# First-norm columns of a decoder layer built by VectorE and through DRAM instead of by TensorE

## The chip, the cores and the metric

One core of one Trainium2 chip runs the whole kernel. The metric is the device time of one execution in microseconds. TensorE (PE) multiplies matrices, VectorE (DVE) and ScalarE (ACT) do the elementwise work, GpSimd (POOL) does a little, and SyncE's queue (SP) issues most transfers. Each engine takes its instructions in the order in which they were written for it, and a waiting instruction holds up all behind it. PE's weight loads are shown as PEld.

## What is computed

One decoder layer over 1024 tokens of 1024 channels, in float32:

```python
z = x @ w_in                                   # pool group | q | k | v
mix = concat(pool_mixer(z), attention(z)) @ w_out
h = layer_norm(ALPHA * x + mix, ln1_g, ln1_b)  # the first norm
ff = square(relu(h @ w_ff1)) @ w_ff2           # hidden width 4096
h = layer_norm(ALPHA * h + ff, ln2_g, ln2_b)
out = h + sigmoid(h @ w_ple_gate + b) * (p @ w_ple)
```

The result of the first norm is used twice: as the residual, with tokens in rows, and as input of `w_ff1`, where the contraction runs over channels. The product wants it in columns: channels on the 128 partitions, tokens along the free axis.

## The kernel before

Each float32 product is made of three matmuls of the reduced type fp32r (lines 113 to 115): an operand is split into a high part (ScalarE, `high`, line 98) and the rest (VectorE, `low`, line 103).

The tokens stand in eight tiles of 128 rows, `hn[0]` to `hn[7]`. For each tile the residual and the products with `w_out` come first (`out_left`, `out_right`, `residual`, line 440), then `norm1(n)`. This normalizes the tile in place (`layer_norm`, lines 402 to 419: its last two steps are L418 and L118 on 128x1024), turns it into columns with eight TensorE transposes of 128x128 into two PSUM banks (`transposed`, line 427; tiles `pt` and `av`), stores ALPHA times the rows to DRAM for later (lines 532 and 533, `hd`), and builds the operands of the feed-forward products from the columns.

The product with `w_ff1` is done by a scheme of seven block products in place of eight (Strassen's, in Winograd's form). Its right operands, over all 1024 tokens, are seven tiles of columns: "11" and "21" are the columns of tiles 0 to 3 (channels 0 to 511 and 512 to 1023); "22", "T1", "T2", "T3" are made from the columns of tiles 4 to 7 and of those; "T4" comes last (`last_sum`). The profile calls "11", "21", "T1", "T2", "T3", "T4" all `c` and "22" `x`; with numbers they are c_335, c_336, c_374, c_375, c_376, c_377 and x7_373. Each is 512 tokens wide, so a matmul on one needs the columns of all four token tiles.

The order around the change: TensorE does `out_left(1)`, the four `out_right` of tiles 4 to 7 (24 matmuls each), then sixteen products of twelve matmuls on "11" and "21" (`early(0)` to `early(7)`: one on "11" and, later, one on "21" for each), and then the main loop, whose first matmuls are on "T2" (PSUM tiles `f`). `norm1(4)` to `norm1(7)` are written between the `early` calls. Within dependences and a bounded set of buffers a scheduler sets each engine's order when the kernel is built. The buffers that matter: `ws` (six of 4 KB per partition: raw weights and their split parts), `w` (two: raw weights), `n` (eight of 4 KB: `hn` and others).

Each of the weight blocks for these products comes by a transfer on SP's queue (line 583 for `early`, 639 for the main loop), is split by ScalarE and VectorE into `ws`, and then loaded as the stationary operand.

Of the kernel before, what the change touches and what calls it, by code (L numbers as in the profile page):

```python
# [67 lines left out]
def layer(ctx, tc, xT, x, pT, w_in, w_pool, pscale, sinks, w_out, ln1, w1, w2, ln2, w_ple, w_gate, bgate, bias, rcount, out):  # L68
    nc = tc.nc
# [6 lines left out]
    def nm(s):  # L76
        uid[0] += 1
        return f"{s}_{uid[0]}"
# [7 lines left out]
    def nat(shape, dt=F32):  # L86
        return sb.tile(shape, dt, tag="n", bufs=8, name=nm("n"))
# [8 lines left out]
    def high(dst, src, scale=None):  # L96
        if scale is None:
            nc.scalar.copy(out=dst, in_=src)  # L98
        else:
            nc.scalar.mul(out=dst, in_=src, mul=scale)  # L100

    def low(eng, dst, src, hi):
        return eng.tensor_tensor(out=dst, in0=src, in1=hi.bitcast(F32), op=ALU.subtract)  # L103
# [13 lines left out]
    def add(o, a, b, op=ALU.add):  # L117
        nc.vector.tensor_tensor(out=o, in0=a, in1=b, op=op)  # L118
# [13 lines left out]


    h_dram = [tc.dram_tile([P, D], F32, name=f"hd{n}") for n in range(NT)]
    f_dram = [tc.dram_tile([P, 2, 2, 2, HALF], F32, name=f"fd{q}") for q in range(NQUAD - NKEEP)]


# [3 lines left out]
    ps = ps_ctx.enter_context(tc.tile_pool(name="ps", bufs=1, space=PSUM))  # L141
# [26 lines left out]
    def tr_ps():  # L168
        return ps.tile([P, 4, P], F32, tag="pt", bufs=2, name=nm("pt"))
# [227 lines left out]
    hn = [None] * NT  # L397

    def layer_norm(y, gb, root=False):
        st = small([P, 2, 6])  # L400
        for i in range(2):
            nc.vector.bn_stats(out=st[:, i, :], in_=y[:, i * HALF : (i + 1) * HALF])
        mv = small([P, 8])
        nc.vector.bn_aggr(out=mv[:, 0:2], in_=st.rearrange("p a b -> p (a b)"))
        v, r0, e, r, m = (mv[:, i : i + 1] for i in range(2, 7))
        nc.vector.tensor_scalar(out=v, in0=mv[:, 1:2], scalar1=LN_EPS, scalar2=None, op0=ALU.add)
        if root:
            nc.vector.reciprocal(out=r0, in_=v)
            nc.scalar.activation(out=r0, in_=r0, func=AF.Sqrt)
        else:  # L410
            nc.gpsimd.tensor_tensor(out=r0, in0=v, in1=mhalf, op=ALU.pow)

        nc.vector.scalar_tensor_tensor(out=e, in0=r0, scalar=v, in1=r0, op0=ALU.mult, op1=ALU.mult)
        nc.vector.tensor_scalar(out=e, in0=e, scalar1=-0.5, scalar2=1.5, op0=ALU.mult, op1=ALU.add)
        nc.vector.tensor_tensor(out=r, in0=r0, in1=e, op=ALU.mult)
        nc.vector.tensor_scalar(out=m, in0=mv[:, 0:1], scalar1=-1.0, scalar2=None, op0=ALU.mult)
        nc.scalar.activation(out=y, in_=y, func=AF.Identity, bias=m, scale=1.0)
        nc.vector.scalar_tensor_tensor(out=y, in0=y, scalar=r, in1=gb[0], op0=ALU.mult, op1=ALU.mult)  # L418
        add(y, y, gb[1])

    def tr_av():
        return ps.tile([P, 4, P], F32, tag="av", bufs=1, name=nm("av"))

    def transposed(y, j, pt):
        for k in range(4):
            kt = 4 * j + k
            nc.tensor.transpose(pt[:, k, :], y[:, kt * P : (kt + 1) * P], ident)  # L427
        return pt
# [77 lines left out]
    def temp(shape=(P, HALF)):  # L506
        return p1.tile(list(shape), F32, tag="t", bufs=6, name=nm("t"))

    def part(shape=(P, 2, 4, P), dt=F32R):
        return p1.tile(list(shape), dt, tag="ws", bufs=6, name=nm("ws"))  # L510

    def wide(tag, shape, dt):
        return p1.tile(shape, dt, tag=tag, bufs=1, name=nm(tag))


    X = {}

    def block(name, i, c):
        return X[name][:, i, :, c * P : (c + 1) * P].bitcast(F32)

    def split_to(name, c, src, eng):
        cs = slice(c * P, (c + 1) * P)
        dh = X[name][:, 0, :, cs]
        high(dh, src)
        return low(eng, X[name][:, 1, :, cs], src, dh)

    def norm1(n):
        t, c = n // 4, n % 4
        layer_norm(hn[n], gb1)
        a = transposed(hn[n], 0, tr_ps())  # L530
        b = transposed(hn[n], 1, tr_av())
        nc.scalar.mul(out=hn[n], in_=hn[n], mul=ALPHA)
        nc.scalar.dma_start(out=h_dram[n], in_=hn[n])
        if t == 0:
            if c < 3:
                nc.scalar.copy(out=pre[:, 4 + c].rearrange("p (k t) -> p k t", k=4), in_=a)
            split_to("11", c, a, nc.vector)
            split_to("21", c, b, nc.vector)
        else:
            r12, t1, t2 = temp((P, 4, P)), temp((P, 4, P)), nat([P, 4, P])  # L540
            nc.scalar.copy(out=r12, in_=a)
            if c < 3:
                add(t1, a, pre[:, 4 + c].rearrange("p (k t) -> p k t", k=4), ALU.subtract)
# [191 lines left out]
    for i in range(len(order) + AHEAD):  # L735
# [9 lines left out]
        p, name = order[i - AHEAD]  # L745
# [91 lines left out]
    for u, (i, q) in enumerate(units):  # L837
        k = QORDER.index(q)
# [133 lines left out]
```

## Time and profile before

| what | value |
| --- | --- |
| median of three timed runs | 994.76 us (994.67 to 995.08) |
| the profiled execution: span from first to last instruction | 993.0 us |
| lies around the span, against the median | 1.8 us |
| PE, DVE, ACT, POOL busy | 985.4, 711.0, 457.9, 105.6 us |
| granted TensorE clock | 1.000 |
| DMA moved | 148.01 MB |

The profiled execution has no time of its own beside its span; the three timed runs agree within 0.04%, so its time is taken as the median, 1.8 us above the span. Busy time is an engine's time in instructions, and idle time of an engine that nothing waits for costs nothing. A row of the timeline gives start, duration, engine, line, operation, tiles and shapes; neighbouring starts on PE are closer than the durations since matmuls overlap in the pipeline.

### The profile page before, as it was taken

What the parts mean: (1) busy time and instruction counts of PE and PEld (TensorE: products, weight loads), DVE (VectorE), ACT (ScalarE), POOL (GpSimd) and SP (SyncE); (2) the same over time, 40 slices, a digit from 0 to 9 for tenths busy, and PEclk for the clock granted to TensorE, in tenths of its full rate; (3) what the DMA queues carried; (4) which work ended last, traced back from release to release, by engine and by line L of the source; (5) the groups of instructions that cost most, each with busy time, mean ns of one, the idle gap of its engine ahead of it and who ended that gap; (6) DMA issues with size and microseconds to landing.
All of it is one profiled execution on the core that took longest, in us unless ns stands there. A gap on an engine that the chain in (4) does not pass through costs nothing.

```text
span 993.0 us, 12231 instructions
## 1 busy us (share of the span) xinstructions
PE 985.4 (99%) x4562; PEld 820.8 (83%) x4562; DVE 711.0 (72%) x1137; ACT 457.9 (46%) x737; POOL 105.6 (11%) x142
## 2 busy tenths in 40 slices
PE   9999999999999999999999999999999999999998
PEld 7888887888888888888888888888888888888887
DVE  5898888895869777564446756887647799896333
ACT  5676766543576443434444434433343454651111
POOL 0013562020000000100000000100111010000000
PEclk9999999999999999999999999999999999999999
DMA  6512142722161543742372993675798863721011
GB/s 218 181 64 85 45 147 85 233 82 89 66 238 57 191 149 149 198 163 106 118 274 96 343 330 101 181 227 201 207 212 186 217 157 118 215 73 43 35 40 43
DMA packets 39004, 148.01 MB, mean 149 GB/s; under 512 B 4768, under 2 KB 5920, under 8 KB 36128
## 3 DMA queue, kind: packets, MB, share of 16 engines
q1 hardware_dynamic: 29520, 115.90, 34.2%
q0 software_dynamic: 7840, 26.74, 11.4%
q10 hardware_dynamic: 1584, 4.59, 1.1%
q8 instruction: 36, 0.59, 0.2%
q14 instruction: 24, 0.20, 0.1%
HBM read 124.66 MB, written 22.54 MB: 148 GB/s over the span
## 4 chain that ended last, share of the span: by engine, by line
PE 98%; DVE 1%; POOL 1%; DMA 0%; issue 0%; ACT 0%; DVEq 0%
PE f L114 23%; PE f L115 23%; PE f L113 23%; PE mm L113 8%; PE mm L115 8%; PE mm L114 8%; PE pt L316 1%; PE s L293 1%; PE s L292 1%; PE f L427 1%; PE av L321 1%; PE av L322 1%; POOL h L360 0%; PE s L113 0%; PE s L114 0%; DMA n<-in_xT 0%
## 5 line engine op out<-in xcount | busy, mean ns | idle before, releaser
L113 PE MATMUL f<-c,ws 128*128 128x512 f32 (+1 forms) x456 | 175.8, 385 | 0.0
L114 PE MATMUL f<-c,ws 128*128 128x512 f32 (+1 forms) x456 | 175.7, 385 | 0.0
L115 PE MATMUL f<-c,ws 128*128 128x512 f32 (+1 forms) x456 | 175.2, 385 | 0.0
L115 PE MATMUL f<-x,w 128*128 128x512 f32 x448 | 174.3, 389 | 0.0
L114 PE MATMUL f<-x,w 128*128 128x512 f32 x448 | 174.3, 389 | 0.0
L113 PE MATMUL f<-x,w 128*128 128x512 f32 x448 | 147.1, 389 | 0.0
L98 ACT CAST w<-st 128x1024 fp32r<-128x1024 f32 (+2 forms) x66 | 65.7, 998 | 109.0 <-issue 69.9
L103 DVE TENSOR_TENSOR w<-st,w 128x1024 fp32r<-128x1024 f32 (+2 forms) x66 | 77.5, 1177 | 48.9 <-ACT w L98 48.8
L113 PEld LDWEIGHTS f<-c,ws 128*128 128x128 f32 x456 | 85.7, 188 | 17.2
L114 PEld LDWEIGHTS f<-c,ws 128*128 128x128 f32 x456 | 85.7, 188 | 17.1
L115 PEld LDWEIGHTS f<-c,ws 128*128 128x128 f32 x456 | 85.7, 188 | 17.1
L115 PEld LDWEIGHTS f<-x,w 128*128 128x128 f32 x448 | 84.1, 188 | 17.5
L114 PEld LDWEIGHTS f<-x,w 128*128 128x128 f32 x448 | 84.1, 188 | 17.5
L113 PEld LDWEIGHTS f<-x,w 128*128 128x128 f32 x448 | 84.0, 188 | 17.4
L98 ACT CAST ws<-w 128x512 fp32r<-128x512 f32 x60 | 37.1, 622 | 57.5 <-PE f L115 42.4
L103 DVE TENSOR_TENSOR x<-ws,x 128x1024 fp32r<-128x1024 f32 x52 | 63.4, 1218 | 0.0
L118 DVE TENSOR_TENSOR n<-t,f 128x512 f32<-128x512 f32 x48 | 31.9, 685 | 39.3 <-PE f L115 39.2
L103 DVE TENSOR_TENSOR ws<-w,ws 128x512 fp32r<-128x512 f32 x60 | 41.1, 689 | 25.1 <-ACT ws L98 24.7
L98 ACT CAST ws<-st 128x512 fp32r<-128x512 f32 x48 | 29.8, 621 | 60.1 <-PE f L115 35.2
L113 PE MATMUL mm<-c,w 128*128 128x512 f32 x144 | 56.4, 396 | 0.3 <-ACT w L98 0.3
L115 PE MATMUL mm<-c,w 128*128 128x512 f32 x144 | 56.5, 394 | 0.0
L114 PE MATMUL mm<-c,w 128*128 128x512 f32 x144 | 56.4, 393 | 0.0
(212 smaller groups left out, 1819.5 us busy)
## 6 DMA issues: line engine op xcount, KB each, us to landing
ws<-in_w SPq DMA_DIRECT2D x70, 512.0 KB, 3.9
w<-in_w SPq DMA_DIRECT2D x16, 1024.0 KB, 5.3
c<-fd SPq DMA_DIRECT2D x6, 2048.0 KB, 8.4
fd<-n POOLq DMA_DIRECT2D x20, 512.0 KB, 3.5
ws<-in_w POOLq DMA_DIRECT2D x20, 512.0 KB, 7.8
st<-in_w_in SPq DMA_DIRECT2D x17, 512.0 KB, 3.3
w<-in_w SPq DMA_DIRECT2D x10, 512.0 KB, 4.1
n<-in_x SPq DMA_DIRECT2D x8, 512.0 KB, 6.0
```

The source lines that it names most:

```text
L98: nc.scalar.copy(out=dst, in_=src)
L103: return eng.tensor_tensor(out=dst, in0=src, in1=hi.bitcast(F32), op=ALU.subtract)
L113: nc.tensor.matmul(o, ah, bh, start=first, stop=False, skip_group_check=more)
L114: nc.tensor.matmul(o, ah, bl, start=False, stop=False, skip_group_check=more)
L115: nc.tensor.matmul(o, al, bh, start=False, stop=last, skip_group_check=more)
L118: nc.vector.tensor_tensor(out=o, in0=a, in1=b, op=op)
L292: nc.tensor.matmul(s[:, i, dst], ql, kt[:, 0, g, kk : kk + kn], start=True, stop=False)
L293: nc.tensor.matmul(s[:, i, dst], ql, kt[:, 1, g, kk : kk + kn], start=False, stop=True)
L316: nc.tensor.transpose(pt[:, i, :], e[:, i, kb * P : (kb + 1) * P], ident)
L321: nc.tensor.matmul(av, VV[0][:, blk, g], pp[:, 0], start=(kb == lo), stop=False)
L322: nc.tensor.matmul(av, VV[0][:, blk, g], pp[:, 1], start=False, stop=(kb == 1))
L427: nc.tensor.transpose(pt[:, k, :], y[:, kt * P : (kt + 1) * P], ident)
```

## The change

`norm1` no longer calls `transposed`. In its place stands `flip`: VectorE transposes the tile in 32x32 pieces in one instruction (128x1024, into a `ws` buffer), SP's queue stores the result to a DRAM scratch (`td0` to `td7`, 512 KB each, 4 KB per partition), and four transfers on the same queue, one for each group of 32 partitions (128 KB each, in runs of 1 KB), read it back in the order that makes columns. The four reads wait for the store. They land in another `ws` buffer for tiles 0 to 3 and in an `n` buffer for tiles 4 to 7. All that read the columns in PSUM now read them there, in views of four by 32 tokens (4x4x32). The second norm (`gate_in`) keeps its TensorE transposes.

```diff
+    t_dram = [tc.dram_tile([P, 4, 2 * P], F32, name=f"td{n}") for n in range(2 * NT)]
...
-    def tr_av():
-        return ps.tile([P, 4, P], F32, tag="av", bufs=1, name=nm("av"))
+    def flip(y, b, t, d):
+        b4 = b.rearrange("p (q k c) -> p q k c", q=4, k=NK)
+        nc.vector.transpose(out=b4, in_=y.rearrange("p (k q r) -> p q k r", k=NK, q=4))
+        nc.sync.dma_start(out=d, in_=b.rearrange("p (q e) -> p q e", q=4))
+        for q in range(4):
+            nc.sync.dma_start(
+                out=t[32 * q : 32 * q + 32].rearrange("r (R e) -> r R e", R=4),
+                in_=d[:, q].rearrange("(R r) e -> r R e", R=4),
+            )
+        return t.rearrange("p (R k c) -> p R k c", R=4, k=NK)
...
+    def columns(name, i, c):
+        return X[name][:, i, :, c * P : (c + 1) * P].rearrange("p k (R c) -> p R k c", R=4)
...
     def norm1(n):
         t, c = n // 4, n % 4
         layer_norm(hn[n], gb1)
-        a = transposed(hn[n], 0, tr_ps())
-        b = transposed(hn[n], 1, tr_av())
+        ft = flip(hn[n], part((P, D), F32), nat([P, D]) if t else part((P, D), F32), t_dram[n])
+        a, b = ft[:, :, 0:4], ft[:, :, 4:8]
         nc.scalar.mul(out=hn[n], in_=hn[n], mul=ALPHA)
...
-                nc.scalar.copy(out=pre[:, 4 + c].rearrange("p (k t) -> p k t", k=4), in_=a)
+                nc.scalar.copy(out=quarters(pre[:, 4 + c]), in_=a)
...
-            r12, t1, t2 = temp((P, 4, P)), temp((P, 4, P)), nat([P, 4, P])
+            r12, t1, t2 = quarters(temp()), quarters(temp()), quarters(nat([P, HALF]))
```

TensorE loses 64 transposes (16 groups of four); the order of its matmuls up to the main loop stays the same but for one exchange inside the early products, and the first product of the main loop is now interrupted after one matmul. In the lists below names carry their numbers: n_349 to n_352 are `hn[4]` to `hn[7]`, n_385, n_402, n_419, n_436 the columns of these four tiles, n_301 is `hn[3]`. In the changed kernel the lines from 420 on are others: L424 is the 32x32 transposition, L425 the store, L427 the reads, L449 the residual (440 before), L597 and L653 the weight loads (583 and 639 before).

SP's queue from the fifth weight block of `early` to the second block of the main loop, before:

```order
L583 DMA w_411_2694<-in_w1 128x1024
L583 DMA w_423_2773<-in_w1 128x1024
L583 DMA w_428_2811<-in_w1 128x1024
L583 DMA w_440_2891<-in_w1 128x1024
L639 DMA w_446_2949<-in_w1 128x2048
L639 DMA w_452_2968<-in_w1 128x2048
```

and now:

```order
L597 DMA w_411_2698<-in_w1 128x1024
L425 DMA td5_88<-ws_401_2635 128x1024
L427 DMA n_402_2636<-td5_88 32x4x256 x4
L597 DMA w_423_2775<-in_w1 128x1024
L597 DMA w_428_2813<-in_w1 128x1024
L425 DMA td6_89<-ws_418_2750 128x1024
L427 DMA n_419_2751<-td6_89 32x4x256 x4
L597 DMA w_440_2891<-in_w1 128x1024
L653 DMA w_446_2949<-in_w1 128x2048
L425 DMA td7_90<-ws_435_2865 128x1024
L427 DMA n_436_2866<-td7_90 32x4x256 x4
L653 DMA w_452_2968<-in_w1 128x2048
```

Between the weight loads stand the stores, which wait for VectorE, and the reads, which wait for the stores.

VectorE from the end of the norm of tile 3 to the first columns, before (mm_339 to mm_341 and s_342 are the results of `out_left(1)`):

```order
L118 TENSOR_TENSOR n_301_1871<-n_301_1871,st_330_2003 128x1024
L440 SCALAR_TENSOR_TENSOR n_349_2232<-n_349_2232,mm_339_2114 128x512
L440 SCALAR_TENSOR_TENSOR n_350_2234<-n_350_2234,mm_340_2115 128x512
L402 BN_STATS sm_382_2498<-n_349_2232 128x6
L440 SCALAR_TENSOR_TENSOR n_351_2236<-n_351_2236,mm_341_2116 128x512
L440 SCALAR_TENSOR_TENSOR n_352_2238<-n_352_2238,s_342_2117 128x512
L103 TENSOR_TENSOR c_335_2110<-pt_355_2254,c_335_2110 128x4x128
L103 TENSOR_TENSOR c_336_2111<-av_356_2259,c_336_2111 128x4x128
```

and now (ws_356 and ws_360 are the columns of tiles 0 and 1):

```order
L118 TENSOR_TENSOR n_301_1887<-n_301_1887,st_330_2019 128x1024
L103 TENSOR_TENSOR c_335_2126<-ws_356_2271,c_335_2126 128x4x4x32
L424 STREAM_TRANSPOSE ws_363_2328<-n_300_1885 128x1024
L103 TENSOR_TENSOR c_336_2127<-ws_356_2271,c_336_2127 128x4x4x32
L449 SCALAR_TENSOR_TENSOR n_349_2248<-n_349_2248,mm_339_2130 128x512
L449 SCALAR_TENSOR_TENSOR n_350_2250<-n_350_2250,mm_340_2131 128x512
L403 BN_STATS sm_382_2506<-n_349_2248 128x6
L449 SCALAR_TENSOR_TENSOR n_351_2252<-n_351_2252,mm_341_2132 128x512
L449 SCALAR_TENSOR_TENSOR n_352_2254<-n_352_2254,s_342_2133 128x512
L103 TENSOR_TENSOR c_335_2126<-ws_360_2300,c_335_2126 128x4x4x32
L424 STREAM_TRANSPOSE ws_367_2357<-n_301_1887 128x1024
L103 TENSOR_TENSOR c_336_2127<-ws_360_2300,c_336_2127 128x4x4x32
```

The transpositions of tiles 2 and 3 stand behind the first uses of the columns of tiles 0 and 1, and that of tile 3 also behind the four residuals.

VectorE where the columns of tile 7 arrive (pt_435 and av_436 before, n_436 now), to the step that makes n_439, from which ScalarE makes the high part of the last quarter of "T2"; before:

```order
L118 TENSOR_TENSOR t_438_2876<-pt_435_2863,c_335_2110 128x512
L103 TENSOR_TENSOR ws_450_2961<-st_447_2951,ws_450_2961 128x512
L118 TENSOR_TENSOR st_447_2951<-w_446_2949,st_447_2951 128x512
L118 TENSOR_TENSOR t_438_2876<-t_438_2876,c_335_2110 128x512
L118 TENSOR_TENSOR n_439_2877<-av_436_2868,t_438_2876 128x512
```

and now:

```order
L118 TENSOR_TENSOR t_438_2876<-n_436_2866,c_335_2126 128x512
L118 TENSOR_TENSOR t_437_2875<-n_436_2866,t_437_2875 128x512
L103 TENSOR_TENSOR x7_373_2479<-n_436_2866,x7_373_2479 128x4x4x32
L118 TENSOR_TENSOR t_438_2876<-t_438_2876,c_335_2126 128x512
L103 TENSOR_TENSOR ws_449_2958<-w_446_2949,ws_449_2958 128x512
L103 TENSOR_TENSOR ws_450_2961<-st_447_2951,ws_450_2961 128x512
L118 TENSOR_TENSOR st_447_2951<-w_446_2949,st_447_2951 128x512
L103 TENSOR_TENSOR c_376_2482<-t_437_2875,c_376_2482 128x4x4x32
L118 TENSOR_TENSOR st_453_2970<-w_452_2968 128x512
L118 TENSOR_TENSOR n_388_2532<-c_336_2127,n_388_2532 128x512
L118 TENSOR_TENSOR n_439_2877<-n_436_2866,t_438_2876 128x512
```

Between the first use of the columns and n_439 stood three rows of 128x512, and now nine.

The rows on VectorE between the steps of the second half, by size, counted in the changed order (a BN_STATS row reads 128x512 and counts as one):

| from, to | 128x512 | 128x1024 | 128x12 or smaller |
| --- | --- | --- | --- |
| "11" of tile 3, up to the transposition of tile 4 | 8 | 2 | 6 |
| behind it, up to the first use of tile 4's columns | 8 | 2 | 8 |
| that use (one row), then the transposition of tile 5 | 1 | | |
| behind it, up to the first use of tile 5's columns | 10 | 2 | 5 |
| two uses, then the transposition of tile 6 | 2 | | |
| behind it, up to the first use of tile 6's columns | 9 | 2 | 2 |
| two uses, then the transposition of tile 7 | 2 | | |
| behind it, up to the first use of tile 7's columns | 11 | | |
| from that use to n_439, both included | 11 | | |

More of the change, by code (lines that the diff above doesn't have):

```diff
@@ L516, in layer, with quarters @@
     X = {}
+    def columns(name, i, c):
+        return X[name][:, i, :, c * P : (c + 1) * P].rearrange("p k (R c) -> p R k c", R=4)
     def block(name, i, c):
-        return X[name][:, i, :, c * P : (c + 1) * P].bitcast(F32)
+        return columns(name, i, c).bitcast(F32)
     def split_to(name, c, src, eng):
-        cs = slice(c * P, (c + 1) * P)
-        dh = X[name][:, 0, :, cs]
+        dh = columns(name, 0, c)
         high(dh, src)
-        return low(eng, X[name][:, 1, :, cs], src, dh)
+        return low(eng, columns(name, 1, c), src, dh)
+    def quarters(t):
+        return t.rearrange("p (R k c) -> p R k c", R=4, k=4)
     def norm1(n):
@@ L539, in norm1 @@
         else:
-            r12, t1, t2 = temp((P, 4, P)), temp((P, 4, P)), nat([P, 4, P])
+            r12, t1, t2 = quarters(temp()), quarters(temp()), quarters(nat([P, HALF]))
             nc.scalar.copy(out=r12, in_=a)
             if c < 3:
-                add(t1, a, pre[:, 4 + c].rearrange("p (k t) -> p k t", k=4), ALU.subtract)
+                add(t1, a, quarters(pre[:, 4 + c]), ALU.subtract)
             else:
```

## Prediction

> **What bounds the kernel now.** The page first, for who is busy, then the chain that ended last.
>
> ```profile
> span 993.0 us, 12231 instructions
> PE 985.4 (99%) x4562; PEld 820.8 (83%) x4562; DVE 711.0 (72%) x1137; ACT 457.9 (46%) x737; POOL 105.6 (11%) x142
> PE 98%; DVE 1%; POOL 1%; DMA 0%; issue 0%; ACT 0%; DVEq 0%
> ```
>
> TensorE is busy for 985.4 of 993.0 us and carries 98% of the chain: what it no longer does is won, unless it then waits. The span is 1.8 us under the median of 994.76; I work within this execution and subtract from the median. Next the table by stretches: `out_right` of tiles 4 to 7, the early products, the first main products.
>
> ```profile
> 234.00:255.90 21.90, 21.90 (x112) 18.34 (x111) 16.98 (x34) 10.24 (x15) 1.10 (x2) 1.00 0.18 73
> 255.90:307.00 51.10, 51.10 (x244) 42.32 (x244) 38.89 (x69) 37.44 (x64) 5.15 (x9) 1.00 0.43 155
> 307.00:335.00 28.00, 28.00 (x125) 23.21 (x124) 24.24 (x40) 12.55 (x21) 1.62 (x3) 1.00 0.34 113
> ```
>
> The columns after the stretch are PE, PEld, DVE, ACT, POOL, clock, DMA share, GB/s. PE never idles here and the clock is 1.00, but VectorE has only 12 us free of 51: it is the second limit, and it gets the work.
>
> **What TensorE loses.** The timeline at both ends of the stretch:
>
> ```profile
> 234.12 0.60 PE L427 MATMUL pt<-ident,n 128*128 128x128 f32 x4
> 306.49 0.39 PE L114 MATMUL mm<-c,ws 128*128 128x512 f32 x1
> 306.72 0.39 PE L115 MATMUL mm<-c,ws 128*128 128x512 f32 x1
> 306.95 0.39 PE L113 MATMUL f<-c,ws 128*128 128x512 f32 x1
> ```
>
> From the first transpose to the first main matmul pass 72.83 us. They hold 4 x 24 + 16 x 12 = 288 matmuls of 128x512, which start every 0.2267 us: 65.3 us. The rest, 7.5 us, is the 64 transposes and the switching around them. Freed of them and never waiting, PE would reach the main loop at 299.4, and the kernel would take 987.3. That is the most the change can win; everything below asks how much is waited away again.
>
> **What the new path costs.** First VectorE's steps:
>
> ```profile
> L103 DVE TENSOR_TENSOR ws<-w,ws 128x512 fp32r<-128x512 f32 x17 | 11.5, 687 | 4.8 <-ACT ws L98 4.6
> L418 DVE SCALAR_TENSOR_TENSOR n<-n,sm,st 128x1024 f32<-128x1024 f32 x8 | 10.2, 1281 | 0.5
> L118 DVE TENSOR_TENSOR n<-n,st 128x1024 f32<-128x1024 f32 x8 | 9.7, 1217 | 0.0
> 293.55 0.68 DVE L103 TENSOR_TENSOR c<-t,c 128x512 fp32r<-128x512 f32 x1
> 294.15 0.68 DVE L118 TENSOR_TENSOR st<-st,w 128x512 f32<-128x512 f32 x1
> L98 ACT CAST ws<-w 128x512 fp32r<-128x512 f32 x11 | 6.9, 624 | 1.4 <-DVE w L118 1.4
> ```
>
> Back to back a 128x512 step takes 0.60 from start to start; a 128x1024 step 1.17, the mean of 1.28 and 1.22 less the same overlap of 0.08; the tiny steps of the norm I set at 0.12. No row shows a 32x32 transposition. Bounds: 1.13, one overlapped pass over 128x1024, and 2.4, two passes. I take 1.2, the row of the same size and type. ScalarE reads columns from SBUF now; a 128x512 cast took 0.62, as good as from PSUM, so I cost that at nothing. The 4x4x32 views too: they have the same element count.
>
> Then the transfers:
>
> ```profile
> hd<-n ACTq DMA_DIRECT2D x8, 512.0 KB, 2.6
> w<-in_w SPq DMA_DIRECT2D x3, 512.0 KB, 4.1
> w<-in_w SPq DMA_DIRECT2D x2, 1024.0 KB, 5.2
> st<-in_w_in SPq DMA_DIRECT2D x17, 512.0 KB, 3.3
> nd<-in_bias SPq DMA_DIRECT2D x1, 128.0 KB, 4.6
> n<-in_x SPq DMA_DIRECT2D x8, 512.0 KB, 6.0
> L846 SPq DMA_DIRECT2D pre<-hd x4: 326/430/439, 582.6 to 584.0; - x4
> ```
>
> A round trip R runs from the end of a transposition to the last read landed. The store is like `hd`: 2.6. The issue costs 0.3, four issues in a row 1.4 (last row: four starts within 1.4 us). The reads: as quick as one quiet 512 KB load, 3.3, and all four at once gives R = 6.2; as slow as the loads of x, 6.0, behind four issues gives 10.3. I take the 4.1 of the weight loads in this very window: R = 2.6 + 0.3 + 1.4 + 4.1 = 8.4.
>
> *First half.* Tiles 0 to 2 have their columns before they matter. Tile 3's transposition now stands behind the four residuals, which wait for `out_left(1)`:
>
> ```profile
> 234.75 0.68 DVE L440 SCALAR_TENSOR_TENSOR n<-n,s 128x512 f32<-128x512 f32 x1
> ```
>
> The next row can start at 235.3; one row and the transposition make 237.1; R and a ScalarE cast (0.6) give 246.1. TensorE wants "11" after four `out_right`, at 234.12 + 21.76 = 255.9. Hidden, with 9 us to spare: the cover is `out_right`. But VectorE waits for those columns in its row, and the residuals and norms of tiles 4 to 7 stand behind it. So 246.1 starts a chain on VectorE.
>
> *Second half*, by the counts in the table of the change (0.60, 1.17 and 0.12 a row). Tile 4's transposition ends at 246.1 + 4.8 + 2.3 + 0.7 + 1.2 = 255.1. Its columns land at 263.5; VectorE gets to them at 263.2 and waits 0.3. Tile 5's ends 1.8 later, 265.3; columns at 273.7, VectorE there at 274.2, no wait. Tile 6's ends 2.4 later, 276.6; columns at 285.0, VectorE there at 284.6. Tile 7's ends at 287.4; columns at 295.8, VectorE there at 294.0: 1.8 of waiting. Eleven rows to n_439, 6.6, and ScalarE's 0.6: "T2" is whole at 303.0. TensorE, without stalls, is there at 299.4 and waits 3.6. Against 306.95 that leaves a gain of 3.9.
>
> *What else is moved.* On SP eight stores and 32 reads now stand between weight loads. The nearest: the second main block (w_452) is issued behind tile 7's reads, about 293; a 1 MB load takes 5.2 here, so 298, and VectorE wants it at 300.6. Free, with 2.4 of cover. Inside the early products the split of the second block (ws_390) stands behind tile 4's transposition and ends about 258.9, and PE wants it at 259.1; a small stall there is paid anyway at the main loop. Behind n_439, 26 VectorE rows of 0.60 lead to the last quarter of "T4": 15.6 us, and PE asks for it 72 matmuls, 16.3 us, after its start; cover 1.3. POOL's power step and its stores keep their number; VectorE can only wait for them 0.6 at a time, as before:
>
> ```profile
> DVE ws L103 <- ACT ws L98: 5.7, 4, 2.0
> DVE c L103 <- ACT c L98: 4.0, 9, 0.7
> DVE sm L413 <- POOL sm L411: 0.6, 1, 0.6
> ```
>
> My sum sets the waits of VectorE on ScalarE at nothing, where the window 234 to 307 now has 9.7 us of them, mostly slack. I add 1.0 us, an estimate of a tenth, for these and T4's thin cover. Forecast: 994.76 - 3.9 + 1.0 = 991.9.
>
> **The rivals.**
>
> *All is hidden (faster still).* With R at 7.0 the waits on transfers vanish: "T2" is whole at 237.1 + 7.6 + 9.0 + 9.9 + 11.35 + 10.4 = 285.35, + 7.0 + 7.2 = 299.6, and the gain is 7.4 less 1.0: 988.4. At R = 6.2, or with no more waits than counted, 987.3. For it speak the quiet loads at 3.3 and the low DMA share, 0.18 and 0.43. Against it the 1 KB runs and four transfers for one. [...]
>
> *The round trip is long (slower).* One mechanism: above 8.4 each added us of R is paid at tile 3, tile 4, tile 6 and tile 7, and partly at tile 5, since VectorE stands at the first use of the columns with the next transposition behind it. It decides from R = 9.1 on, where "T2" comes at 306.0 and the 1.0 eats the rest. At R = 10: 247.7, 256.7, 268.5, 280.9, 293.3, then 303.3 + 7.2 = 310.5: 994.76 + 3.6 + 1.0 = 999.4. For it speak x's 6.0 and the 4.6 of the lone 128 KB read in 1 KB rows; against it that these fell where the queues were full.
>
> *The transposition costs two passes (slower).* At 2.4, tiles 3 to 7 each add 1.2 to the same chain: 6.0, so 991.9 + 6.0 = 997.9. The trace has nothing for or against. [...]
>
> **How the numbers follow.** The forecast 40%; hidden 20%; long round trip 28%; two passes 12%. A stall of TensorE in the first half gets none of its own: 237.1 + R + 0.6 reaches 255.9 only with R at 18. The likeliest alone spans 990.0 to 994.5 (R from 8 to 9). A measurement of this kernel can tell about 0.2%, 2 us: faster means under 992.8, slower above 996.7. Faster: 0.27 of the forecast's 0.40 and all of the hidden case, 0.47. Same: 0.13, 0.08 of the long trip, 0.02 of the two passes, 0.23. Slower: 0.20 + 0.10 = 0.30. The range runs from 987.3, all hidden, to 999.4, a trip of 10; beyond lie the longest of the long trips, and both mishaps together, under 2 in 10.
>
> **What would show it.** Right: PE rows of line 427 fall from 128 to 64; eight VectorE rows near 1.2 us; `td` stores near 2.6 us; reads within 5.8 us of the first issue; PE idle only just ahead of the first `f` matmul, for 3 to 5 us, released by ScalarE's cast to `c`; afterwards no idle. Wrong: PE idle inside the early products beyond 1 us, VectorE waiting for DMA at t for more than 2 us a tile, transpositions above 1.6 us, or any wait at `c` for T4. The sum fails if VectorE stalls on ScalarE more than I allowed, since from 246 to 303 it has almost no free time.

## The result and the profile after

The changed kernel takes 1000.25 us (median of four runs, 999.21 to 1002.44) against 994.87 us before: 5.4 us slower, ratio 1.0059, interval 1.0047 to 1.0071. The prediction was 991.9 us in a range up to 999.4: the side was wrong, and the time lies outside the range. (Ratios and intervals, here and below, are those on record; they need not be the quotient of the two medians.) The execution with the profile below took 1002.44 us (span 1000.6), the longest of the four, so its terms add up to 2.2 us more than the median.

First the page of the changed kernel: span, busy time, chain.

```profile
span 1000.6 us, 12177 instructions
PE 983.1 (98%) x4498; PEld 815.7 (82%) x4498; DVE 718.5 (72%) x1145; ACT 459.1 (46%) x737; POOL 107.9 (11%) x142
PE 87%; DMA 5%; DVE 4%; issue 1%; ACT 1%; SPq 1%; POOL 0%; DVEq 0%; ACTq 0%; POOLq 0%
```

TensorE carried 98% of the chain; now transfers and VectorE have 9%. The table by stretches says where (columns as before: PE, PEld, DVE, ACT, POOL, clock, DMA share, GB/s).

```profile
214.00:234.00 20.00, 20.00 (x89) 16.26 (x87) 11.24 (x16) 4.94 (x6) 0.55 (x1) 1.00 0.76 242
234.00:256.00 22.00, 20.49 (x91) 16.93 (x91) 16.37 (x31) 8.78 (x13) 0.56 (x1) 1.00 0.65 211
256.00:307.00 51.00, 45.24 (x193) 36.24 (x192) 44.79 (x80) 37.84 (x66) 9.31 (x9) 0.95 0.67 237
307.00:335.00 28.00, 26.14 (x104) 20.95 (x103) 22.45 (x37) 12.44 (x22) 1.62 (x3) 0.90 0.30 113
```

TensorE is idle in three of the four, the clock is below 1.00 in the last two, and the DMA share in 256 to 307 is 0.67 where 0.43 stood. In 214 to 234 the queues move 242 GB/s, 4.84 MB; in the kernel before it was 132 GB/s, 2.64 MB:

```profile
214.00:234.00 20.00, 20.00 (x90) 16.57 (x89) 13.04 (x21) 4.01 (x7) 2.73 (x1) 1.00 0.41 132
```

The timeline of PE in the changed kernel shows the waits one by one (the bracket is the idle time ahead and its releaser).

```profile
235.55 0.50 PE L113 MATMUL mm<-c,c 128*128 128x512 f32 x1 [1.51 <-DVE n L449]
261.75 0.50 PE L115 MATMUL mm<-c,ws 128*128 128x512 f32 x1 [0.95 <-DVE ws L103]
299.74 0.39 PE L115 MATMUL mm<-c,ws 128*128 128x512 f32 x1
304.93 0.80 PE L113 MATMUL mm<-c,ws 128*128 128x512 f32 x1 [4.81 <-ACT pre L601]
305.53 0.63 PE L114 MATMUL mm<-c,ws 128*128 128x512 f32 x1
305.95 0.63 PE L115 MATMUL mm<-c,ws 128*128 128x512 f32 x1
311.70 0.73 PE L113 MATMUL f<-c,ws 128*128 128x512 f32 x2 [1.86 <-ACT c L98]
316.15 0.40 PE L115 MATMUL f<-c,ws 128*128 128x512 f32 x1
```

The main loop starts at 311.70 in place of 306.95: 4.75 us. From 311.70 to 316.15 stand twelve steps that take 4.45 us where 12 x 0.2267 = 2.72 would do: 1.73 us, at a start every 0.43 us, with the granted clock at 0.50 from 312.4 to 315.9. Together 6.5 of the 7.6 us by which the span grew; the other 1.1 fall later, 0.77 of it in one wait at 647.15 that the kernel before does not have. Now what held it up, on VectorE (the transpositions of tiles 0, 3 and 7, and its waits at columns; T0 in what follows is 248.79, its first row on tile 3's columns):

```profile
214.84 1.24 DVE L424 STREAM_TRANSPOSE ws<-n 128x1024 f32<-128x1024 f32 x1
232.48 0.69 DVE L103 TENSOR_TENSOR c<-ws,c 128x512 fp32r<-128x512 f32 x1 [8.55 <-ACT c L98]
238.48 1.24 DVE L424 STREAM_TRANSPOSE ws<-n 128x1024 f32<-128x1024 f32 x1
248.79 0.69 DVE L103 TENSOR_TENSOR c<-ws,c 128x512 fp32r<-128x512 f32 x1 [2.28 <-ACT c L98]
289.73 0.69 DVE L118 TENSOR_TENSOR t<-n,pre 128x512 f32<-128x512 f32 x1 [2.08 <-DMA n<-td]
290.97 1.24 DVE L424 STREAM_TRANSPOSE ws<-n 128x1024 f32<-128x1024 f32 x1
302.24 0.69 DVE L118 TENSOR_TENSOR t<-n,c 128x512 f32<-128x512 f32 x1 [2.67 <-DMA n<-td]
```

A transposition takes 1.24. Tile 0's ends at 216.1, yet its columns are not used before 231.3 (ScalarE's first row below): a trip of 15.2 us. Tile 7's ends at 292.2, and its columns are there at 302.2: 10.0. On ScalarE:

```profile
231.30 0.62 ACT L550 COPY pre<-ws 128x512 f32<-128x512 f32 x1 [9.42 <-DMA ws<-td]
302.22 0.62 ACT L555 COPY t<-n 128x512 f32<-128x512 f32 x1 [3.44 <-DMA n<-td]
304.30 0.58 ACT L601 COPY pre<-mm 128x512 f32<-128x512 f32 x1
309.88 0.60 ACT L591 ACTIVATE t<-mm 128x512 f32<-128x512 f32 x1 [2.29 <-PE mm L115]
311.05 0.60 ACT L98 CAST c<-n 128x512 fp32r<-128x512 f32 x1
```

This is a chain across three engines. The copy L601 takes a finished sum out of a PSUM bank, so that the last early product can add onto that bank, and it stands behind the copies and casts for tile 7's columns. The product starts at 304.93 at half speed (a start every 0.43 us, the granted clock at 0.50 from 302.2 to 309.0) and so takes 4.9 us; its relu (L591) waits for it; the cast of T2's last quarter (311.05), whose input VectorE had ready at 309.0, stands behind the relu; TensorE waits for that cast.

### The profile page after: what moved, and what is told of

The parts are those of the page before. It is cut to its first block, busy times and chain, and to the rows that moved or that the text cites. A ratio compares the mean times of both kernels' runs of the same rounds, so it can differ in the third digit from the quotient of the medians.

```text
span 1000.6 us, 12177 instructions
## 1 busy us (share of the span) xinstructions
PE 983.1 (98%) x4498; PEld 815.7 (82%) x4498; DVE 718.5 (72%) x1145; ACT 459.1 (46%) x737; POOL 107.9 (11%) x142
## 4 chain that ended last, share of the span: by engine, by line
PE 87%; DMA 5%; DVE 4%; issue 1%; ACT 1%; SPq 1%; POOL 0%; DVEq 0%; ACTq 0%; POOLq 0%
PE f L114 22%; PE f L115 22%; PE f L113 22%; PE mm L113 5%; PE mm L115 5%; PE mm L114 5%; DMA td<-ws 2%; DMA ws<-in_w 1%; DMA n<-td 1%; PE pt L317 1%; PE s L294 1%; PE s L293 1%; PE f L436 1%; DVE x L103 1%; SPq L427 1%
## 5 line engine op out<-in xcount | busy, mean ns | idle before, releaser
L113 PE MATMUL f<-c,ws 128*128 128x512 f32 (+1 forms) x456 | 176.4, 387 | 1.9 <-ACT c L98 1.9
L113 PE MATMUL f<-x,w 128*128 128x512 f32 x448 | 147.1, 389 | 0.0
L113 PEld LDWEIGHTS f<-c,ws 128*128 128x128 f32 x456 | 86.0, 189 | 19.6 <-ACT c L98 2.3
L113 PEld LDWEIGHTS f<-x,w 128*128 128x128 f32 x448 | 84.0, 188 | 17.5
L113 PE MATMUL mm<-c,w 128*128 128x512 f32 x144 | 56.1, 394 | 0.4 <-ACT w L98 0.4
L98 ACT CAST x<-ws 128x1024 fp32r<-128x1024 f32 x52 | 54.5, 1048 | 0.0
```

The costliest lines, as they stand in the source:

```text
L113: nc.tensor.matmul(o, ah, bh, start=first, stop=False, skip_group_check=more)
```

## Experiments

In kernels called held, a table of ordering edges (which wait for nothing) keeps every engine's instructions in the order of the changed kernel; it adds 19 to the line numbers (L132 is L113). In the others the scheduler orders anew. Every run is compared with runs of the kernel before on its own chip (medians 994.59 to 994.91).

**The halves apart.** (`t == 1` in second_half_only; the other tiles as in the kernel before.)

```diff
-        ft = flip(hn[n], b_tile, f_tile, t_dram[n])
+        if t == 0:
+            ft = flip(hn[n], b_tile, f_tile, t_dram[n])
+        else:
+            a, b = transposed(hn[n], 0, tr_ps()), transposed(hn[n], 1, tr_av())
```

> Tiles 0 to 3 take the new path, tiles 4 to 7 go back to TensorE's eight transposes. Theory A (the loss comes from the second half, where ScalarE and VectorE stand at the first use of the columns with the rest queued behind): half of the 7.5 us of transposes is won, the first half costs its two short stalls of TensorE (1.5 and 0.95 us), no stall of several us ahead of the main loop and no clock under 1.00 there: 991 to 994.5 us. Rival C (the loss starts with the crowded transfers of the first half, which pass 2.7 us of lateness on to all that follows): TensorE still stalls 2 us or more ahead of the main loop and the time is 996 or above.

> Tiles 4 to 7 take the new path, tiles 0 to 3 go back to TensorE's transposes. Theory A: the round trips of tiles 6 and 7 and the stall behind them stay; TensorE waits 3 to 7 us ahead of the main loop, at a lower clock behind the wait: 997 to 1000 us. Rival C: without the crowd of the first half the columns of tile 7 come some 3 us earlier, TensorE waits under 2 us, and the time is 991 to 994.

Measured: tiles 0 to 3 alone 993.07 us (ratio 0.9984, 0.9976 to 0.9993); tiles 4 to 7 alone 998.18 (1.0023, 1.0009 to 1.0036), its single runs spread from 993.9 to 1000.3. Half of the 7.5 us should have given 991.0 each: the first half loses 2.1 of it, the second 7.2. Added to the best case of 987.3 they make 996.6; both together take 1000.25, 3.7 us more. That the one half makes the other late would explain these 3.7, but they are a difference of medians of which one spreads over 6 us. In the profile of the second half alone (its longest execution, 1000.25) tile 7's trip takes 12.1 us with no transfers of the first half beside it, and TensorE waits at the same place:

```profile
305.71 0.79 PE L113 MATMUL mm<-c,ws 128*128 128x512 f32 x1 [5.51 <-ACT pre L607]
```

**The waits taken away, the bytes kept.** Held. First the reads take their bytes from the input, so that they don't wait for the store; then they also stand ahead of the store on SP's queue.

```diff
-                in_=d[:, q].rearrange("(R r) e -> r R e", R=4),
+                in_=src[:, 256 * q : 256 * q + 256].rearrange("(R r) e -> r R e", R=4),
```

> The changed kernel with the orders of all engines held; the four reads of each tile take their bytes from the input x, in the same shapes and runs, so that they don't wait for the store (the true columns are left out; the store stays). The trip loses the store's 2.4 to 3 us. Theory A (long round trip, paid at tiles 3, 6 and 7): tile 7's columns come at 294 to 297 in place of 302.2, TensorE's stalls ahead of the main loop shrink from 6.7 to under 1.5 us, and the time is 991 to 994. Rival V (VectorE's and ScalarE's own order and rows set the end; the trip is only where they are seen to wait): TensorE's main loop starts later than 308 and the time is 997 or above.

> As reads_without_store, orders held, and on SP's queue each tile's four reads stand ahead of its store, so that nothing waits for a transfer that starts after the transposition: a trip of about nothing. All bytes are still moved. Theory A (VectorE and ScalarE wait for the trip): what reads_without_store left of stalls, 2.2 us in the first half and 1.9 us with half clock ahead of the main loop, goes too; TensorE reaches the main loop at 299.5 to 302 without a wait of over 1 us: 987.5 to 990.5. Rival V (VectorE's rows, with the four transpositions added, don't fit ahead of T2): main loop from 304 on, 992.5 or more.

Measured: 994.97 us (1.0010, 0.9995 to 1.0026; single runs from 993.8 to 1000.8), then 990.31 (0.9961, 0.9948 to 0.9974). (Both kernels leave out the true columns: the reads bring other data.) The first shows theory A only in direction: 5.3 us fewer, 1 us above the range; a wait of 2.2 us of TensorE at 236.7 stayed, and with it the half clock (a start every 0.43 us from 238.0 to 241.0). In its profile tile 0's reads, which wait for no store, still land 15.9 us behind the transposition (216.5 to 232.5): they are issued behind other loads by 222.6, and the last takes some 10 us more. So here the loads beside them do it, on the queue and in the transfer. The second is within the expectation and decides: with as many bytes and every instruction still there, waiting for the round trip, together with what stands behind that wait on SP's queue, costs 9.9 us: all of the loss, and more than half of the 7.5 us that the change can win. What is left of TensorE's waits from 210 to 335 is one row, and VectorE's load with eight transpositions is no obstacle:

```profile
301.29 0.74 PE L132 MATMUL f<-c,ws 128*128 128x512 f32 x2 [1.86 <-ACT c L117]
```

This wait is for the cast of T2 behind the last early product, and it stands here without any trip to wait for. With it the main loop starts 1.9 us behind the best case's 299.4, and 1.1 us fall later: the 3.0 by which 990.3 misses 987.3.

**How the columns are read.** Held; one transfer of 512 KB in runs of 4 KB in place of four.

> Orders as in the changed kernel; each tile's columns are read back by one transfer of 512 KB in runs of 4 KB, not four of 128 KB in runs of 1 KB (the true arrangement of the columns is left out). Theory T (four issues and 1 KB runs make the read slow): the trip falls from 8.5 to 10 us to 6 to 7.5, as in reads_without_store the stalls ahead of the main loop shrink to 2 us or less, 993 to 996 us. Rival Q (the bytes of the weight loads and hd stores in flight at that time set it, however it is read): trips of 8 us and more at tiles 6 and 7, 998 us or more.

Measured: 998.49 us (1.0027, 1.0014 to 1.0041), single runs from 993.9 to 999.9. 1.8 us fewer: nearer to rival Q. Its profile is of its fastest execution (993.86), with trips of 8.8 and 7.5 us for tiles 6 and 7; those of its slower executions are in no trace. Four issues and short runs are a part of the trip's cost; by the median not its core.

**The clock, and the last early product.** Held. Matmuls of no use keep TensorE busy in its two waits (18 or 9 of them in the second); or the last product gets a bank of its own.

```diff
+        if p == NPRE: warm(20)
         rest()
+        if p == NPRE: warm(18)
```

> The changed kernel with every engine's order held; 20 added matmuls of 128x512 into an idle PSUM bank ahead of the last early product and 18 behind it, so that TensorE is busy where it waited 4.8 and 1.9 us. Theory B (the clock that falls in the wait lies on the path: the last early product takes 4.9 us where 12 x 0.2267 = 2.7 would do, ScalarE's relu of it and the cast of T2's last quarter stand behind that, and the main loop's first 4 us run at half speed): main loop starts about 309.7 to 310 in place of 311.7 and runs at 0.2267 from its first matmul: 4 us less than the changed kernel, about 996 us. Rival V (T2's last quarter is late by VectorE's chain alone and TensorE's speed changes nothing before it): main loop still starts at 311.7, only the half speed behind it is saved: 998 us. Rival N (the lower clock costs nothing, its time is waited anyway): 1000 us.

> As warm_in_the_waits, but 9 added matmuls behind the last early product in place of 18. There T2's last quarter was cast by 309.4 (311.65 in the changed kernel), but the 18 kept TensorE until 311.4. Theory B: TensorE is free at about 307.3 + 9 x 0.2267 = 309.4, the main loop starts at 309.4 to 309.9 at full clock: 2 us less than with 18, about 997.5 us, so that the fallen clock costs some 2.5 to 3 us of the changed kernel's 1000.2. Rival N: 999.5 again, the clock's time is waited elsewhere.

> Orders of all engines as in the changed kernel; the last early product goes to a PSUM bank of its own, so that it no longer waits for ScalarE's copy out of the bank (the sum of the two products is left out). Theory D (the stall of 4.8 us ahead of that product is ScalarE's copy, which stands behind the copies of tile 7's columns; the product's lateness then delays the cast of T2 behind its relu): no wait at the last early product, T2's cast at about 309 in place of 311; TensorE waits about 7 us in one piece ahead of the main loop and pays 2 us of half clock there: 998 us. Rival: the copy is only where the wait is seen and T2 comes at 311.7 whatever the product does: 1000 us.

Measured: 999.55 us (1.0051, 1.0039 to 1.0063), 999.06 (1.0049, 1.0037 to 1.0061), 1000.83 (1.0060, 1.0048 to 1.0072). Theory B missed its size, and theory D its time. The profile of warm_in_the_waits shows that the mechanism of B is there:

```profile
304.56 0.50 PE L132 MATMUL mm<-c,ws 128*128 128x512 f32 x1 [0.73 <-ACT pre L620]
308.79 0.60 ACT L117 CAST c<-n 128x512 fp32r<-128x512 f32 x1
311.49 0.72 PE L132 MATMUL f<-c,ws 128*128 128x512 f32 x2
```

The product took 2.9 us, T2's cast came 2.3 us sooner than in the changed kernel, and the clock was 1.00; but the 18 matmuls were too many and kept TensorE until 311.4. With 9 the gain was 1.2 us in the median, and its interval overlaps that of the changed kernel. The traces say more. From the copy of tile 7's columns to the first matmul of the main loop and to the thirteenth it takes 9.5 and 13.9 us in the changed kernel, but 7.6 and 10.4 with 20 and 9 matmuls:

```profile
304.21 0.62 ACT L574 COPY t<-n 128x512 f32<-128x512 f32 x1 [3.83 <-DMA n<-td]
311.81 0.72 PE L132 MATMUL f<-c,ws 128*128 128x512 f32 x2
```

So in the traces the half clock costs 3.5 us, the late product and the main loop's start together. The median shows only 1.2: in this profiled execution tile 7's columns came 2.0 us later than in the changed kernel, and why is not shown. With a bank of its own the product ran on time, T2's cast came at 309.2, and TensorE waited 6.7 us in one piece, with half clock behind it (a start every 0.43 us from 310.9 to 313.0):

```profile
302.15 0.63 ACT L574 COPY t<-n 128x512 f32<-128x512 f32 x1 [3.29 <-DMA n<-td]
309.83 1.22 PE L132 MATMUL f<-c,ws 128*128 128x512 f32 x2 [6.69 <-ACT c L117]
```

That is theory D's mechanism, and with tile 7's columns at the same time as in the changed kernel the main loop starts 1.9 us sooner; but the medians (1000.83 and 1000.25) show no gain, so what the copy L601 costs stays open.

**Using the columns later.** A tile's use of its columns is written behind the norm and transposition of the next tile, in the second half.

> Second half rewritten: a tile's use of its columns is written behind the norm and the transposition of the next tile (order 4, 5, use 4, 6, use 5, 7, use 6, use 7), the scheduler orders the rest. Nothing is left out. Theory A (VectorE and ScalarE, in order, stand at the first use of the columns while the next tile's norm is queued behind): they no longer wait for the columns there, T2 is whole by 302 to 305, TensorE waits under 2 us ahead of the main loop: 990.5 to 994. Rival L (VectorE's own rows, 45 of 51 us, fill the stretch, so that order gains nothing): T2 at 308 or later, 997 or more.

Measured: 1002.41 us (1.0071, 1.0058 to 1.0084); the expectation is wrong also in that something is left out, since the copy in `pre` that tile 6 subtracts is overwritten first. Theory A as stated here fell. Tile 7's transposition ended at 285.0, 7 us sooner, and T2 came no sooner. SP's queue says why (start and duration of the issue, tiles, count):

```profile
281.77 2.43 SPq L604 DMA_DIRECT2D w<-in_w  x2
285.00 1.17 SPq L426 DMA_DIRECT2D td<-ws  x1
290.54 1.98 SPq L428 DMA_DIRECT2D n<-td  x4
292.62 3.78 SPq L661 DMA_DIRECT2D w<-in_w  x2
```

The store follows 1 MB of weights and takes 5.5 us until its reads may start, and the main loop's weights stand behind those. VectorE waits 1.98 at 299.6 for these weights, ahead of T2's rows: the wait has moved from the columns to the weights.

**Why the first trips take 15 us.** Two candidates: the bytes beside them, or SP's queue, in which a tile's reads wait for their store with the next store behind them. First the later use of the columns in the first half, alone and with all tiles on the new path (`front` is the norm, the transposition, the transfers and the scaling, `back_after` the uses of the columns, behind the last residual):

```diff
-    for n in range(4):
-        norm1(n)
-    residual_left(1, os)
+    for n in range(3):
+        front(n)
+    last = residual_left(1, os)
+    back_after(0, 2); front(3)
+    for n in range(1, 4):
+        back_after(n, 3)
```

> first_half_only (tiles 4 to 7 on TensorE), with the first use of the columns of tiles 0 to 3 held behind the norms and transpositions of tiles 0 to 2 and behind the four residuals on VectorE, so that VectorE no longer stands 8.6 us at the columns of tile 0 with the residuals behind it. Theory C1 (that stall, not the bytes, is what the first half loses): the 0.9 us wait of TensorE for a residual goes and T0 comes earlier: 991.0 to 992.3, against 993.07. Rival C2 (the first half's remaining 2 us are lost elsewhere, in VectorE's rows or in later waits): 992.7 to 993.5.

> The same late use in the first half, with tiles 4 to 7 on the new path as in the changed kernel. If the first half's lateness passes on to T2 in full (theory C1), T0 comes 2 to 3 us earlier than 248.8 and the time falls by as much: 996.5 to 998.5. If the trips of tiles 6 and 7 set T2 by themselves: 999.5 to 1001.

Measured: 994.08 us (0.9995, 0.9985 to 1.0005; single runs from 991.3 to 996.9) and 1004.35 (1.0088, 1.0074 to 1.0103), both above the expected ranges. Theory C1 fell: VectorE no longer stood at tile 0, but the columns came no sooner. In late_use_all tile 2 was transposed by 225.2, and SP's queue:

```profile
222.22 0.43 SPq L428 DMA_DIRECT2D td<-ws  x1
232.95 2.17 SPq L430 DMA_DIRECT2D ws<-td  x4
235.21 0.42 SPq L428 DMA_DIRECT2D td<-ws  x1
```

Tile 1's store was 10.7 us under way, its reads waited for it, and tile 2's store stood behind them until 235.2. Then the two candidates one at a time, the bytes in the changed kernel (held, two weight loads of 512 KB put off on SP's queue), the queue in late_use_all (the stores issued by ScalarE):

> The changed kernel, orders of all engines held but for one thing: on SP's queue the two weight loads of 512 KB that stood between the transfers of tiles 0 and 1 stand behind the reads of tile 3 and the two weight loads that are needed first. Theory C (bytes in flight): the store of tile 1, 10 us to landing in the changed kernel, lands 1 to 2.5 us sooner, VectorE's wait of 8.6 us at tile 0's columns shrinks by as much, and about that passes on: 998 to 999.2 us. Theory E (the queue's own order): 999.8 to 1000.5.

> late_use_all with the eight td stores on ScalarE's queue, just ahead of the step that scales the same rows; the reads stay on SP's. Bytes unchanged. Theory E: the stores of tiles 2 and 3 no longer stand behind the reads of tiles 1 and 2 (issued 235.2 and 241.7 there, 10 and 4 us after their transposition), tile 3's columns come 3 to 5 us sooner than 250.2 and the time falls from 1004.35 to 999 to 1001.5. Theory C: the crowd alone sets the landings, 1003 to 1005.

Measured: 998.48 us (1.0033, 1.0020 to 1.0045), 1.8 below the changed kernel, and 999.92 (1.0052, 1.0039 to 1.0064), 4.4 below late_use_all. Both play a part. Without the two loads VectorE's wait of 8.55 at tile 0 is 5.12, but T0 is no sooner (249.06 for 248.79), since tile 3's trip grew to 10.8 us:

```profile
229.29 0.69 DVE L122 TENSOR_TENSOR c<-ws,c 128x512 fp32r<-128x512 f32 x1 [5.12 <-ACT c L117]
249.06 0.69 DVE L122 TENSOR_TENSOR c<-ws,c 128x512 fp32r<-128x512 f32 x1 [3.45 <-ACT c L117]
```

TensorE's wait of 1.51 is gone in it and tile 7's columns come 1.5 us sooner (300.7); which of the two gives the 1.8 us is not shown.

With the stores on ScalarE, tile 3's columns came only 1.8 us sooner (248.4 for 250.2), where theory E had 3 to 5. The first early weights, which stood behind the reads of tile 3 on SP, were issued 3.9 us sooner, and a wait of TensorE for their cast is gone:

```profile
262.46 0.71 PE L113 MATMUL mm<-c,ws 128*128 128x512 f32 x1 [3.82 <-ACT ws L98]
```

In late_use_all that cast stands on ScalarE behind the scaling of tile 4, whose transposition ended at 260.8 there and at 256.9 here. How much of these 3.9 us comes from the weights and how much from the columns is not shown.

**Both together.** Late use, weights put off, for tiles 0 to 3 alone; then also the stores on ScalarE; then that for all tiles; then that with the later use in the second half, too.

```diff
-        nc.sync.dma_start(out=d, ...)
+        nc.scalar.dma_start(out=d, ...)
...
+        with tc.issue_after(last_read[3].ins):
             nc.sync.dma_start(out=r, in_=w1[p, :, 0:2])
```

> late_use_first_half, and the weight loads for the early products (1 MB of them fell between the transfers of tiles 0 and 1) stand behind the reads of tile 3 on SP's queue. Theory C (the bytes in flight make the first trips 15 us long): the stores and reads of tiles 0 and 1 land 1 to 2.5 us sooner; the time changes only as far as those columns are still waited for: 990.5 to 992, and 0.3 to 1 us under late_use_first_half. Rival: no difference of over 0.3 us, since the late use already covers the trip.

> late_use_quiet (tiles 0 to 3 on the new path, weight loads behind) with the td stores on ScalarE's queue. Theory E on top of C: 991.0 to 992.0, 0.4 to 1.4 us under late_use_quiet's 992.37. If late_use_quiet has no wait left that matters: 992.0 to 992.7.

> The same for all eight tiles. The first half's lateness should be gone (T0 at 244 to 246 in place of 248.8); tiles 6 and 7 keep trips of 8 to 10 us in the second half. Theory A: main loop still waits 2 to 5 us and pays its half clock, 995 to 998. If the second half was late only through T0: 990 to 993.

> quiet_scalar_all, and in the second half a tile's use of its columns is written behind the norm and the transposition of the next one or two tiles (4, 5, use 4, 6, use 5, 7, use 6, use 7), the copies of earlier columns used before they are overwritten. Theory A (the wait at the first use of the columns, with the next norm behind it, is what the second half loses): TensorE's wait of 3.1 us ahead of the last early product goes and the main loop starts 2.5 to 5 us sooner: 991 to 993.5. Rival E2 (the weight loads, now behind later stores and reads on the queues, become the wait, as in columns_one_tile_later): 995.5 or more, with VectorE or ScalarE waiting for w.

Measured: 992.37 us (0.9976, 0.9967 to 0.9984); 991.46 (0.9967, 0.9955 to 0.9980); 996.03 (1.0012, 1.0003 to 1.0021); 999.38 (1.0048, 1.0034 to 1.0061). The second is the best version found, 3.1 us below the kernel before and within 0.6 of what half the change can give; TensorE never waits in the stretch:

```profile
256.00:307.00 51.00, 51.00 (x242) 42.36 (x241) 43.28 (x78) 37.61 (x65) 7.04 (x10) 1.00 0.46 165
```

For all tiles the second half's loss stays, as theory A had it: 4.6 us more than with the first half alone, though the new path should take 3.75 off. T0 came 4.7 us sooner than in the changed kernel (244.1), but little of it reached tile 7:

```profile
287.11 0.62 ACT L98 CAST x<-n 128x512 fp32r<-128x512 f32 x1 [3.78 <-DMA n<-td]
288.27 0.33 ACTq L428 DMA_DIRECT2D td<-ws  x1
299.94 0.62 ACT L570 COPY t<-n 128x512 f32<-128x512 f32 x1 [1.22 <-DMA n<-td]
302.65 0.50 PE L113 MATMUL mm<-c,ws 128*128 128x512 f32 x1 [3.10 <-ACT pre L617]
307.10 0.61 PE L113 MATMUL f<-c,ws 128*128 128x512 f32 x2
```

Tile 7 was transposed by 285.1. Its store stood on ScalarE's queue behind the wait for tile 6's columns and was issued 3.2 us later; the trip took 14.9 us. Stores on ScalarE are thus held by waits for columns as those on SP are by waiting reads (in late_use_all tile 2's store, from 225.2 to 235.2). And the main loop did not wait for T2, whose last cast ended at 304.6: the last early product waited 3.10 us for the copy out of its bank and ran at half clock (a start every 0.43 us from 303.3 to 306.3). The last run made it worse by 3.4 us. There tile 7's store was issued 2.4 us behind its transposition, and T2 is again late with no column to wait for: TensorE waited 4.07 us at 307.78, and VectorE has the sums of the main loop's weights ahead of T2's rows and waited 1.51 us for those weights, issued behind tile 7's reads. That supports rival E2; it was not undone by itself.

## Why the prediction was wrong, step by step

- *What TensorE loses, 7.5 us:* right as far as the runs reach. Without waits for the trip 4.3 us of it are won (990.3), and half of the change, mended, wins 3.1 of 3.75.
- *A transposition at 1.2 us:* right, 1.24. The rival of two passes is dead.
- *"Tiles 0 to 2 have their columns before they matter":* this step failed. Their trips took 15.2, 15.9 and 7.6 us, with 4.84 MB moved in 214 to 234 where 2.64 were before. VectorE stood 8.55 us at tile 0's, the residuals behind it came late (TensorE waited 1.51), tile 3's transposition ended at 239.7 in place of 237.1 and T0 was 248.8 in place of 246.1: 2.7 us. That the loads beside the trips and SP's queue lengthen them, reads_without_store, quiet_held and late_use_all show; but no run takes off these 2.7 us by themselves: in quiet_held T0 is as late (249.1), and in first_half_only, with T0 at 248.5, TensorE waits for nothing from 236 to 335, so the lateness does no harm there. With the stores on ScalarE, unneeded loads put off and the columns used later, the same tiles give 991.46.
- *R = 8.4:* right or generous for tiles 3, 4 and 5 (8.4, 7.0, 8.3), too small for 6 and 7 (9.9 and 10.0). The 4.1 for the reads was a load's time in the window before, with a DMA share of 0.43; in the new one, with 0.67, a read of tile 7 takes up to 5.7 to landing. With what it passes on, this term is 3.7 us: T0's 2.7 of lateness has become 6.4 at tile 7's columns (302.2 for 295.8). That the trips as a whole are the cause is shown by reads_ahead_of_store, which takes the wait for them away and 9.9 us with it; the split into 2.7 and 3.7 is read from one profile.
- *"T2" 7.2 us behind the columns:* mis-sized by 2.2 (311.65 for 302.2 + 7.2 = 309.4). The sum counted VectorE's rows and one cast, not that the cast stands in ScalarE's queue behind the relu of a product that itself waits behind tile 7's copies. Nor was a wait inside the early products foreseen: TensorE stood 4.81 us ahead of the last one, and the half clock behind this wait made that product 4.9 us long where it takes 2.7. In two traces in which it ran at the full clock (warm_20_and_9 and quiet_held) the main loop starts 7.6 us behind the columns' copy, not 9.5; so most of the 2.2 is the clock, too, and ScalarE's order alone adds some 0.3 to 0.4 (an estimate from these rows).
- *The clock:* not in the sum at all. 1.73 us in the profile behind the main loop's start, and with the late product 3.5 us in all. The runs that kept TensorE busy won 0.7 and 1.2 us in the median with overlapping intervals, so its price in the time is not settled.
- *The allowance of 1.0:* its size came out by luck. It was for VectorE waiting on ScalarE and for T4; T4 was never waited for, and of the 1.1 us that fall after the main loop's start 0.77 is one wait at 647.15.

The sum with these: 991.9 - 1.0 + 2.7 + 3.7 + 2.2 + 1.7 + 1.1 = 1002.3, the profiled execution's 1002.4, and 2.2 above the median. Two of the prediction's own signs of being wrong appeared: TensorE stood inside the early products (4.81 us), and VectorE waited over 2 us for columns at two tiles (2.08 and 2.67). "The round trip is long" was the nearest rival, 999.4 at R = 10, and reads_ahead_of_store shows its mechanism; but R was 10 only at tiles 6 and 7, and the first half, which the prediction held to be harmless, had the longest trips. "All is hidden" is what would come if nothing waited; it has R at 7.0 or below, and the trips of the changed kernel's trace took 7.0 to 15.9.

What stays open: which bytes or which order make the trips of tiles 6 and 7 long, why tile 7's columns come at different times in executions with the same order, and whether an order exists in which all eight tiles gain. Of the versions tried for it, quiet_scalar_all lost to a store held on ScalarE and a bank that came free late, and the last moved the wait from the columns to the weights. Two variants of quiet_scalar_all that aim at what its trace shows were not run: a bank of its own for the last early product, and the stores of tiles 4 to 7 left on SP.

## What to carry to other kernels

A round trip through DRAM is priced in the window as it will be with the added bytes, not by the loads of the old one, and each of its transfers is followed along its queue: here reads that waited for their store held back the next store and the loads behind them (in late_use_all tile 2's store by 10 us). Where an in-order engine first uses what comes back, ask what stands behind that instruction; a wait there is paid by everything queued (here VectorE's 8.55 us at tile 0's columns, with the residuals behind it), and taken away at one place it can reappear at the next, as in columns_one_tile_later (VectorE's 1.98 us for weights). Of a change made in several places, try the places apart: here half of it, with its stores on another queue and unneeded loads put off, gains 0.3%, and the whole loses 0.6%.

## What was not expected of the hardware

After some waits of TensorE matmuls start every 0.43 us instead of 0.2267 for some us. In the changed kernel the granted clock is 0.50 from 302.2, inside the wait of 4.81 us, to 309.0 (6.8 us), and from 312.4, behind the wait of 1.86 us, to 315.9 (3.4 us). It does not take a long wait: in reads_without_store it fell behind one of 2.20 us, and only 1.3 us after work had begun again (rows between these are left out).

```profile
236.71 0.50 PE L132 MATMUL mm<-c,c 128*128 128x512 f32 x1 [2.20 <-DVE n L468]
237.75 0.46 PE L133 MATMUL mm<-c,c 128*128 128x512 f32 x1
238.44 0.63 PE L132 MATMUL mm<-c,c 128*128 128x512 f32 x1
241.40 0.39 PE L133 MATMUL mm<-c,c 128*128 128x512 f32 x1
```

Nor does the length of the wait decide by itself. Behind the wait of 1.86 us ahead of the main loop the clock fell in the changed kernel, in reads_without_store and in quiet_held (means of 0.90, 0.95 and 0.94 from 307 to 335), and stayed at 1.00 in reads_ahead_of_store. In quiet_held it stayed at 1.00 behind a longer one:

```profile
303.41 0.50 PE L132 MATMUL mm<-c,ws 128*128 128x512 f32 x1 [3.34 <-ACT pre L620]
308.28 1.05 PE L132 MATMUL f<-c,ws 128*128 128x512 f32 x2 [1.86 <-ACT c L117]
```

The time of a transfer to landing is not settled by its shape: in the changed kernel the same 512 KB `td` store took from 2.6 to 10.0 us.
